# A row softmax on one core: edge columns in eight-row transfers, a written order of work, and the scaling on VectorE

## The chip, the cores and the metric

The kernel runs on one core of one Trainium2 chip. The metric is the device time in microseconds. Before the change it was 2495.66 us, the median of three runs from 2494.19 to 2496.56.

The core's engines work side by side and meet only at semaphores. VectorE (DVE in the profile) and ScalarE (ACT) compute, SyncE (SP) issues the transfers here, and 16 DMA engines move the data between the device memory and the on-chip memory of 128 partitions. TensorE does nothing in this kernel, and GpSimd only sets four constants at the start.

## The reference

The input is 16 x 256 rows of 32768 fp32 values, 4096 rows in all, 536.87 MB. The output has the same shape and type. The temperature is 1.0.

```python
def reference(logits, temperature):
    scaled = logits / temperature
    scaled = scaled - scaled.max(axis=-1, keepdims=True)
    exp_scaled = np.exp(scaled)
    return (exp_scaled / exp_scaled.sum(axis=-1, keepdims=True)).astype(np.float32)
```

## The kernel before

Each row is cut into two halves of 16384 columns, and a half row takes one partition, so that partitions 2r and 2r+1 hold the halves of one row. 128 half rows make a group; there are 64 groups (`G`). A group is worked in two chunks (`C`) of 128 x 8192 values, 4 MB each, so there are 128 chunks, numbered 0 to 127 here. Six buffers of a chunk each (`_BUFS`) hold them. A chunk is loaded into its buffer, changed in place, and stored from it.

For each chunk, `exps` has VectorE find the negated maximum of each partition (line 107, into `nm`), and ScalarE take the exponential with that maximum as bias and add up the results (line 114, the sum into `ssum`). After the two chunks of a group, `factors` puts them together: VectorE takes the extreme of the two maxima (line 129), `combine` swaps neighbouring partitions with a shuffle (line 84) and joins the two (line 87), ScalarE takes the exponentials of the differences (`ee`, line 131), VectorE multiplies them with the sums and adds (line 138), `combine` swaps and joins once more, this time the sums, and a reciprocal (line 149) and a product (line 150) give the factor `f` of each chunk. Then `scales` multiplies the chunk by its factor, the left 4096 columns on VectorE (line 160), the right 4096 on ScalarE (line 163).

All loads (line 64) and stores (line 75) are issued from SyncE, one after the other in the order of the list `order` (lines 170 to 174): six loads, store 0, then store i followed by load i+5. A load waits until the store that last read its buffer, store i-1, has landed. The chunks of the first and the last group are loaded in two pieces of 4096 columns; in the last group the maxima, the exponentials, the scaling and the stores are cut in the same way. The semaphores and the order of the instructions on VectorE and ScalarE are the framework's: `factors` is marked as having priority (line 128).

Of the kernel before, what the change touches and what calls it, by code (L numbers as in the profile page):

```python
# [6 lines left out]


_SPLIT = 2
_CW = 8192  # L10
_BUFS = 6
_PIECE = 8192
_LAST_DMA = 4096
_DVE_SHARE = 0.5


@with_exitstack
def kernel(
    ctx: ExitStack,
    tc: tile.TileContext,  # L20
    logits: bass.AP,
    temperature: bass.AP,
    out: bass.AP,
):
    nc = tc.nc
    inv_t = 1.0 / float(temperature)
    P = nc.NUM_PARTITIONS
    fp32 = mybir.dt.float32
    Exp = mybir.ActivationFunctionType.Exp
    Copy = mybir.ActivationFunctionType.Copy  # L30
    X = mybir.AxisListType.X
    A = mybir.AluOpType

    xf = logits.flatten_outer_dims()
    of = out.flatten_outer_dims()
    N, V = xf.shape
    W = V // _SPLIT
    CW = min(_CW, W)
    C = W // CW
    assert W * _SPLIT == V and CW * C == W and (N * _SPLIT) % P == 0  # L40
    x = xf.rearrange("n (h v) -> (n h) v", h=_SPLIT)
    o = of.rearrange("n (h v) -> (n h) v", h=_SPLIT)
    G = N * _SPLIT // P
    n_chunks = G * C
    n_rounds = _SPLIT.bit_length() - 1

    xpool = ctx.enter_context(tc.tile_pool(name="x", bufs=_BUFS))
    spool = ctx.enter_context(tc.tile_pool(name="stats", bufs=3))
    slots = {}
    stats = {}  # L50

    def spans(total: int, step: int) -> list[tuple[int, int]]:
        return [(s, min(step, total - s)) for s in range(0, total, step)]

    def piece(g: int) -> int:
        return _PIECE if g < G - 1 else min(_PIECE, _LAST_DMA)

    def load(i: int) -> None:
        g, c = divmod(i, C)
        xs = xpool.tile([P, CW], fp32, tag="x", name="xs")  # L60
        slots[i] = xs
        for s, n in spans(CW, _LAST_DMA if g in (0, G - 1) else CW):
            tc.keep_in_program_order(
                nc.sync.dma_start(  # L64
                    out=xs[:, s : s + n],
                    in_=x[g * P : (g + 1) * P, c * CW + s : c * CW + s + n],
                )
            )

    def store(i: int) -> None:  # L70
        g, c = divmod(i, C)
        xs = slots.pop(i)
        for s, n in spans(CW, _LAST_DMA if g == G - 1 else CW):
            tc.keep_in_program_order(
                nc.sync.dma_start(  # L75
                    out=o[g * P : (g + 1) * P, c * CW + s : c * CW + s + n],
                    in_=xs[:, s : s + n],
                )
            )

    def combine(v, op) -> None:
        for j in range(n_rounds):
            mask = [i ^ (1 << j) for i in range(32)]
            nc.vector.stream_shuffle(  # L84
                out=v[:, j + 1 : j + 2], in_=v[:, j : j + 1], mask=mask
            )
            nc.vector.tensor_tensor(  # L87
                out=v[:, j + 1 : j + 2],
                in0=v[:, j : j + 1],
                in1=v[:, j + 1 : j + 2],  # L90
                op=op,
            )

    def exps(i: int) -> None:
        g, c = divmod(i, C)
        xs = slots[i]
        ps = spans(CW, piece(g))
        K = C * len(ps)
        if c == 0:
            stats[g] = tuple(  # L100
                spool.tile([P, K], fp32, tag=f"{nm}{K}", name=nm)
                for nm in ("nm", "ssum", "ee", "f", "ttj")
            )
        nm, ssum = stats[g][:2]
        for j, (s, n) in enumerate(ps):
            k = c * len(ps) + j
            nc.vector.tensor_reduce(  # L107
                out=nm[:, k : k + 1], in_=xs[:, s : s + n], axis=X, op=A.max, negate=True
            )
            if inv_t != 1.0:  # L110
                nc.vector.tensor_scalar_mul(
                    out=nm[:, k : k + 1], in0=nm[:, k : k + 1], scalar1=inv_t
                )
            nc.scalar.activation(  # L114
                out=xs[:, s : s + n],
                in_=xs[:, s : s + n],
                func=Exp,
                bias=nm[:, k : k + 1],
                scale=inv_t,
                accum_out=ssum[:, k : k + 1],  # L120
            )

    def factors(g: int) -> None:
        nm, ssum, ee, f, ttj = stats[g]
        nMh = spool.tile([P, 1 + n_rounds], fp32, tag="nMh", name="nMh")
        Sh = spool.tile([P, 1 + n_rounds], fp32, tag="Sh", name="Sh")
        rS = spool.tile([P, 1], fp32, tag="rS", name="rS")
        with tc.high_priority():
            nc.vector.tensor_reduce(out=nMh[:, 0:1], in_=nm, axis=X, op=A.min)  # L129
            combine(nMh, A.min)  # L130
            nc.scalar.activation(  # L131
                out=ee,
                in_=nm,
                func=Exp,
                bias=nMh[:, n_rounds : n_rounds + 1],
                scale=-1.0,
            )
            nc.vector.tensor_tensor_reduce(  # L138
                out=ttj,
                in0=ee,  # L140
                in1=ssum,
                scale=1.0,
                scalar=0.0,
                op0=A.mult,
                op1=A.add,
                accum_out=Sh[:, 0:1],
            )
            combine(Sh, A.add)
            nc.vector.reciprocal(out=rS, in_=Sh[:, n_rounds : n_rounds + 1])  # L149
            nc.vector.tensor_scalar_mul(out=f, in0=ee, scalar1=rS)  # L150

    def scales(i: int) -> None:
        g, c = divmod(i, C)
        xs = slots[i]
        f = stats[g][3]
        ps = spans(CW, piece(g))
        for j, (s, n) in enumerate(ps):
            k = c * len(ps) + j
            cut = int(n * _DVE_SHARE) // 512 * 512
            nc.vector.tensor_scalar_mul(  # L160
                out=xs[:, s : s + cut], in0=xs[:, s : s + cut], scalar1=f[:, k : k + 1]
            )
            nc.scalar.activation(  # L163
                out=xs[:, s + cut : s + n],
                in_=xs[:, s + cut : s + n],
                func=Copy,
                scale=f[:, k : k + 1],
            )

    order = [("L", i) for i in range(min(_BUFS, n_chunks))] + [("S", 0)]  # L170
    for i in range(1, n_chunks):
        order.append(("S", i))
        if i + _BUFS - 1 < n_chunks:
            order.append(("L", i + _BUFS - 1))

    nxt = 0
    done = -1
    loaded = 0
    for kind, i in order:
        if kind == "L":  # L180
            load(i)
            loaded = i + 1
        else:
            g = i // C
            if g > done:
                while nxt < (g + 1) * C:
                    assert nxt < loaded
                    exps(nxt)
                    nxt += 1
                factors(g)  # L190
                done = g
            scales(i)
            store(i)


# [33 lines left out]
```

## Time and profile before

| | |
|---|---|
| time, median of three runs | 2495.66 us |
| profiled execution: span | 2493.8 us |
| bytes read and written | 536.87 MB each |
| mean rate over the span | 431 GB/s |
| maximum of a chunk, line 107, VectorE | 8.68 us each |
| exponential of a chunk, line 114, ScalarE | 7.12 us each |
| scaling of half a chunk, line 160, VectorE | 2.35 us each |
| scaling of half a chunk, line 163, ScalarE | 3.70 us each |
| load of 4 MB, issue to landing, median | 29.0 us |
| store of 4 MB, issue to landing, median | 38.2 us |

The span is the time from the first to the last instruction of one execution as the hardware profiler recorded it; the time of a run holds a little more than the span. The page gives the busy time of each engine, the share of the 16 DMA engines' time in which they moved packets, and the chain of work that ended last. Groups of instructions are named by line, engine, operation and operands, with the number of instructions, busy time and mean length, and the idle time of the engine ahead of them with what ended it. The DMA share in a window is a mean over the 16 engines, so that 0.50 can mean that eight of them are working. "SPq" is SyncE's own queue, where the issue of a transfer takes 0.34 to 0.53 us and stands behind whatever SyncE waits for.

### The profile page before, as it was taken

The page shows a single profiled execution, that of the slowest core. Times are in us where ns is not written, and L with a number is a line of the kernel's source. Part 1 is how long each engine was busy: PE and PEld are TensorE (multiplying, and loading weights), DVE is VectorE, ACT ScalarE, POOL GpSimd, SP SyncE. Part 2 cuts the span into 40 slices and gives each one's busy share as a digit, 9 for nine tenths or more (in the row PEclk, how much of TensorE's full clock was granted, in tenths as well). Part 3 has the DMA queues.
Part 4 walks back from the last instruction along what each step waited for, and adds up shares of the span by engine and source line. Part 5 has one row for each costly group of instructions (what it writes and reads, how often), then busy time and mean ns, then how long its engine had stood idle before and what let it go on. Part 6 is the DMA issues. An engine that isn't in the chain of part 4 may idle for free.

```text
span 2493.8 us, 2234 instructions
## 1 busy us (share of the span) xinstructions
DVE 1487.4 (60%) x964; ACT 1405.0 (56%) x455; POOL 0.2 (0%) x4
## 2 busy tenths in 40 slices
DVE  7655565556655566555665566655666566655663
ACT  5665554655556555565555655555546555465553
POOL 0000000000000000000000000000000000000000
DMA  9999999999999999999999999999999999999998
GB/s 412 433 430 432 429 431 432 433 433 434 433 434 432 435 432 435 432 435 431 436 431 435 432 434 433 434 433 433 433 433 433 433 433 434 434 433 434 432 431 368
DMA packets 37745, 1073.90 MB, mean 431 GB/s; under 512 B 4192, under 2 KB 4192, under 8 KB 4192
## 3 DMA queue, kind: packets, MB, share of 16 engines
q1 hardware_dynamic: 37728, 1073.76, 99.9%
q14 instruction: 17, 0.14, 0.0%
HBM read 536.87 MB, written 536.87 MB: 431 GB/s over the span
## 4 chain that ended last, share of the span: by engine, by line
DMA 96%; SPq 1%; ACT 1%; DVE 1%; issue 1%; ACTq 0%
DMA out_dram<-xs 93%; DMA xs<-in_logits_dram 2%; SPq L64 1%; DVE nm L107 1%; ACT xs L163 1%; ACT xs L114 0%; ACTq L224 0%; SPq L75 0%; DVE f L150 0%; ACT ee L131 0%; DVE rS L149 0%; DVE Sh L87 0%; DVE ttj L138 0%; DVE Sh L84 0%; DVE Sh L138 0%
## 5 line engine op out<-in xcount | busy, mean ns | idle before, releaser
L114 ACT ACTIVATE xs<-xs,nm 128x8192 f32<-128x8192 f32 (+1 forms) x130 | 912.1, 7016 | 972.4 <-DVE nm L107 972.4
L107 DVE TENSOR_REDUCE nm<-xs 128x1 f32<-128x8192 f32 (+1 forms) x130 | 1111.6, 8551 | 527.3 <-DMA xs<-in_logits_dram 527.3
L163 ACT ACTIVATE xs<-xs,f 128x4096 f32<-128x4096 f32 (+1 forms) x130 | 468.1, 3648 | 71.4 <-DVE f L150 71.4
L160 DVE TENSOR_SCALAR xs<-xs,f 128x4096 f32<-128x4096 f32 (+1 forms) x130 | 295.7, 2318 | 3.7 <-DVE f L150 1.8
L138 DVE CUSTOM_DVE_ANT_0 ttj<-ee,ssum 128x2 f32<-128x2 f32 x64 | 10.3, 161 | 423.8 <-ACT ee L131 423.8
L114 ACT ACTIVATION_READ_ACCUMULATOR xs<-xs,nm 128x1 f32 x130 | 24.2, 186 | 0.0
L131 ACT ACTIVATE ee<-nm,nMh 128x2 f32<-128x2 f32 x64 | 17.9, 280 | 0.0
L150 DVE TENSOR_SCALAR f<-ee,rS 128x2 f32<-128x2 f32 x64 | 14.6, 229 | 2.2
L149 DVE RECIPROCAL rS<-Sh 128x1 f32<-128x1 f32 x64 | 10.5, 164 | 2.2
L87 DVE TENSOR_TENSOR nMh<-nMh 128x1 f32<-128x1 f32 x64 | 10.2, 160 | 2.2
L87 DVE TENSOR_TENSOR Sh<-Sh 128x1 f32<-128x1 f32 x64 | 10.2, 160 | 2.2
L129 DVE TENSOR_REDUCE nMh<-nm 128x1 f32<-128x2 f32 x64 | 9.9, 155 | 2.2
L84 DVE STREAM_SHUFFLE nMh<-nMh 128x1 f32<-128x1 f32 x64 | 9.7, 151 | 0.0
L84 DVE STREAM_SHUFFLE Sh<-Sh 128x1 f32<-128x1 f32 x64 | 9.7, 151 | 0.0
L114 ACT ACT_TABLE_LOAD x1 | 1.3, 1283 | 12.9 <-DMA xs<-in_logits_dram 12.9
L138 DVE DVE_READ_ACCUMULATOR2_ANT Sh<- 128x1 f32 x64 | 5.3, 84 | 0.0
L84 DVE LOAD_MASK_SELECT Sh<-Sh x64 | 0.9, 14 | 2.8
L84 DVE LOAD_MASK_SELECT nMh<-nMh x64 | 0.9, 14 | 2.7
L210 POOL MEMSET const-bfloat16-1.0<- 128x1 bf16 x1 | 0.1, 102 | 0.0
L210 POOL MEMSET const-uint8-127<- 128x1 uint8 x1 | 0.1, 102 | 0.0
L210 POOL MEMSET const-float32-0.0<- 128x1 f32 x1 | 0.1, 99 | 0.2 <-issue 0.2
L210 POOL MEMSET const-float32-1.0<- 128x1 f32 x1 | 0.1, 99 | 0.0
## 6 DMA issues: line engine op xcount, KB each, us to landing
out_dram<-xs SPq DMA_DIRECT2D x126, 4096.0 KB, 38.2
xs<-in_logits_dram SPq DMA_DIRECT2D x124, 4096.0 KB, 29.0
xs<-in_logits_dram SPq DMA_DIRECT2D x8, 2048.0 KB, 22.3
out_dram<-xs SPq DMA_DIRECT2D x4, 2048.0 KB, 26.7
```

What stands on the lines that cost most here:

```text
L64: nc.sync.dma_start(out=xs[:, s : s + n], in_=x[g * P : (g + 1) * P, c * CW + s : c * CW + s + n],)
L84: nc.vector.stream_shuffle(out=v[:, j + 1 : j + 2], in_=v[:, j : j + 1], mask=mask)
L87: nc.vector.tensor_tensor(out=v[:, j + 1 : j + 2], in0=v[:, j : j + 1], in1=v[:, j + 1 : j + 2], op=op,)
L107: nc.vector.tensor_reduce(out=nm[:, k : k + 1], in_=xs[:, s : s + n], axis=X, op=A.max, negate=True)
L114: nc.scalar.activation(out=xs[:, s : s + n], in_=xs[:, s : s + n], func=Exp, bias=nm[:, k : k + 1], scale=inv_t, accum_out=ssum[:, k : k + 1],
L129: nc.vector.tensor_reduce(out=nMh[:, 0:1], in_=nm, axis=X, op=A.min)
L131: nc.scalar.activation(out=ee, in_=nm, func=Exp, bias=nMh[:, n_rounds : n_rounds + 1], scale=-1.0,)
L138: nc.vector.tensor_tensor_reduce(out=ttj, in0=ee, in1=ssum, scale=1.0, scalar=0.0, op0=A.mult, op1=A.add, accum_out=Sh[:, 0:1],)
L149: nc.vector.reciprocal(out=rS, in_=Sh[:, n_rounds : n_rounds + 1])
L150: nc.vector.tensor_scalar_mul(out=f, in0=ee, scalar1=rS)
L160: nc.vector.tensor_scalar_mul(out=xs[:, s : s + cut], in0=xs[:, s : s + cut], scalar1=f[:, k : k + 1])
L163: nc.scalar.activation(out=xs[:, s + cut : s + n], in_=xs[:, s + cut : s + n], func=Copy, scale=f[:, k : k + 1],)
```

## The change

The function is written anew, outside the framework's scheduling.

- Every engine's instructions stand in the order in which they are written, and each wait is written out by `Stream.wait`. Each engine has a semaphore of its own that counts its instructions; each buffer has semaphores of its own for its loads and its stores (`Landing`).
- In a group VectorE does, in this order: the maxima of both chunks; after the last exponential one shuffle that swaps maxima and sums together; the extreme over both halves; after `ee` the product-sum over both halves; the reciprocal; the scaling of both chunks. There is one exchange between the partitions in place of two, and no product `f`.
- The scaling is one VectorE instruction for the whole chunk with two scalar operands, `ee` and the reciprocal. ScalarE scales nothing.
- SyncE issues six loads, then for each group, after its stores in order, load i+4 behind store i. Load i+4 goes into the buffer that store i-2 read.
- The last 2048 columns of chunk 5 (the sixth) are loaded by 16 transfers, each of 8 partitions that are 4 apart, all on one semaphore of that buffer. The first 6144 columns are one transfer.

```diff
-    order = [("L", i) for i in range(min(_BUFS, n_chunks))] + [("S", 0)]
-    for i in range(1, n_chunks):
-        order.append(("S", i))
-        if i + _BUFS - 1 < n_chunks:
-            order.append(("L", i + _BUFS - 1))
...
+    for i in range(_BUFS):
+        load(i)
+    for g in range(G):
+        compute(g)
+        for c in range(C):
+            i = g * C + c
             store(i)
+            j = i + _LEAD
+            if j >= _BUFS and j < n_chunks:
+                load(j)
+    sp.wait(*[s.token() for s in stores])
```

Inside `load`, with `_NARROW` = 2048 and `_LEAD` = 4:

```diff
+        b = i % _BUFS
+        sp.wait(*freed[b])
+        pieces = spans(_CW, _EDGE if g in (0, G - 1) else _CW)
+        narrow = _NARROW if i == _BUFS - 1 else 0
+        if narrow:
+            pieces = [(0, _CW - narrow)]
...
+            for q in range(0, P, 32):
+                for r in range(4):
+                    a = q + r
+                    lane.add(
+                        nc.sync.dma_start(
+                            out=X[a : a + 29 : 4, b * _CW + s : (b + 1) * _CW],
+                            in_=x[g * P + a : g * P + a + 29 : 4, c * _CW + s : (c + 1) * _CW],
+                        )
+                    )
```

The exchange and the scaling, in `compute`. Here `t` holds the maxima and then the sums of a group's pieces, `K` of each, and `tv` is a view of it that separates own and neighbour's, maxima and sums:

```diff
+        dve.wait(sums[-1])
+        sh = dve.done(
+            nc.vector.stream_shuffle(out=t[:, 2 * K : 4 * K], in_=t[:, 0 : 2 * K], mask=swap)
+        )
+        dve.wait(sh)
+        mx = dve.done(
             nc.vector.tensor_reduce(
+                out=r[:, 0:1], in_=tv[:, :, 0, :], axis=mybir.AxisListType.XY, op=A.min
+            )
+        )
+        act.wait(mx)
...
+        dve.wait(tr)
+        rc = dve.done(nc.vector.reciprocal(out=r[:, 2:3], in_=r[:, 1:2]))
+        dve.wait(rc)
+        for c in range(C):
...
+                scaled[i, s] = dve.done(
+                    nc.vector.tensor_scalar(
+                        out=xs,
+                        in0=xs,
+                        scalar1=e[:, k : k + 1],
+                        scalar2=r[:, 2:3],
+                        op0=A.mult,
+                        op1=A.mult,
+                    )
+                )
```

And the helper that every wait goes through; a value that the engine has already waited for is not waited for again:

```diff
+    def wait(self, *tokens):
+        need = {}
+        for t in tokens:
+            for sem, value in t if isinstance(t, list) else [t]:
+                key = id(sem)
+                if value > max(self.seen.get(key, 0), need.get(key, (None, 0))[1]):
+                    need[key] = (sem, value)
+        for key, (sem, value) in need.items():
+            self.engine.wait_ge(sem, value)
+            self.seen[key] = value
```

## The prediction

> **What bounds the kernel now.** I read the page first, then the stretches of the span in windows, then the end in 1 us windows, then the queue of SyncE and the first 90 us in order of time.
>
> ```profile
> span 2493.8 us, 2234 instructions
> DVE 1487.4 (60%) x964; ACT 1405.0 (56%) x455; POOL 0.2 (0%) x4
> q1 hardware_dynamic: 37728, 1073.76, 99.9%
> DMA out_dram<-xs 93%; DMA xs<-in_logits_dram 2%; SPq L64 1%; DVE nm L107 1%; ACT xs L163 1%; ACT xs L114 0%; ACTq L224 0%; SPq L75 0%; DVE f L150 0%; ACT ee L131 0%; DVE rS L149 0%; DVE Sh L87 0%; DVE ttj L138 0%; DVE Sh L84 0%; DVE Sh L138 0%
> ```
>
> The transfers are 99.9% of the span of 16 DMA engines, and the chain that ended last is 93% store. VectorE and ScalarE, at 60% and 56%, are not the bound. So only two things can move the end: the rate of the DMA engines, and how evenly the sixteen reach the last byte. The windows (columns: stretch, length, DVE busy, ACT busy, POOL busy, clock, DMA share, GB/s):
>
> ```profile
> 62.00:150.00 88.00, 54.13 (x40) 58.90 (x21) 0.00 (x0) 1.00 1.00 431
> 150.00:470.00 320.00, 190.39 (x121) 175.38 (x56) 0.00 (x0) 1.00 1.00 431
> 470.00:1000.00 530.00, 320.80 (x210) 299.74 (x97) 0.00 (x0) 1.00 1.00 433
> ...
> 2481.00:2482.00 1.00, 0.00 (x0) 0.00 (x0) 0.00 (x0) 1.00 0.96 410
> 2482.00:2483.00 1.00, 0.00 (x0) 0.00 (x0) 0.00 (x0) 1.00 0.50 213
> 2485.00:2486.00 1.00, 0.00 (x0) 0.00 (x0) 0.00 (x0) 1.00 0.42 180
> 2487.00:2488.00 1.00, 0.00 (x0) 0.00 (x0) 0.00 (x0) 1.00 0.15 66
> 2491.00:2492.00 1.00, 0.00 (x0) 0.00 (x0) 0.00 (x0) 1.00 0.08 33
> ```
>
> The steady rate is 433 GB/s: 1073.74 MB would take 2479.8 us, and from a first byte near 2.5 us the end would be 2482.3. At that very time the share drops to 0.50: eight of sixteen engines are done, two are left at 2487.5 (0.15 x 16), one at 2491.5. The last engine is some 10 us behind the first eight. The ten 1 us shares after 2482 (0.50, 0.54, 0.42, 0.42, 0.19, 0.15, 0.12, 0.04, 0.08, 0.08) add up to 2.5, so level engines would end near 2484.5, 7.5 us earlier. That uneven end is all there is to gain. Most of it comes from the first fifth: 431 instead of 433 over 88 and 320 us is 0.4 + 1.5 = 1.9 us for the mean engine, three quarters of the 2.5.
>
> Profile and times: the span is 1.9 us below the median of the runs (2495.66) and 0.4 below the lowest. I add 1.9 to each span I work out.
>
> **Part 1: written order and earlier stores in the queue.** Before, load i+5 follows store i and waits for store i-1; after, load i+4 follows store i and waits for store i-2. A wait at the head of SyncE holds all behind it, stores and loads. Steadily, when load 2g+1 has landed, four transfers stand ahead of store 2g (store, load, store, load; 4 x 4.194 MB / 433 = 38.7 us). The store needs a maximum, an exponential, the exchange and one scaling, for which the rows are:
>
> ```profile
> L107 DVE TENSOR_REDUCE nm<-xs 128x1 f32<-128x8192 f32 x126 | 1094.0, 8682 | 523.4 <-DMA xs<-in_logits_dram 523.4
> L114 ACT ACTIVATE xs<-xs,nm 128x8192 f32<-128x8192 f32 x126 | 897.2, 7121 | 965.1 <-DVE nm L107 965.1
> L160 DVE TENSOR_SCALAR xs<-xs,f 128x4096 f32<-128x4096 f32 x126 | 290.8, 2350 | 3.7 <-DVE f L150 1.8
> ```
>
> 8.7 + 7.1 + 0.2 (accumulator read) + 1.25 + 4.5 = 21.8 us, 17 us in hand: cost 0. At the end, behind the last load only stores 124 and 125 (19.4 us) cover the last group's first store, which needs 4.4 + 3.7 + 0.2 + 1.3 + 2.4 = 12.0 for its halves of a chunk: 7 in hand, cost 0. If that cover went, the queue would run dry and each us late would be a us of span.
>
> **Part 2: one exchange.** Two shuffles, two tensor_tensor and the product f (0.15 + 0.15 + 0.16 + 0.16 + 0.23) go; one wider shuffle and a reduction over both halves come. Before, from the last accumulator read of a group (end 85.91) to the end of f (87.15) is 1.24 us with 0.2 per small step; after, shuffle, maximum, ee (0.28), product-sum (0.22), reciprocal, with a hop each way, are about 1.25. Gain 0: it lies beside DMA. The written waits sit before small steps that waited for their predecessor already; the rows' 0.2 steps include that.
>
> **Part 3: scaling on VectorE alone.** 128 copies of 3.7 us leave ScalarE. VectorE scales 8192 columns: 2 x 2.35 less one start, 4.5 us. The form with two scalar operands is not in the trace. Bounds: 4.5 at the pace of L160, 8.7 at that of L107 (one element per cycle, the same columns). L160 is the nearer row, same operation and operand kinds, so 4.5. VectorE's group in its written order is 2 x 8.7 + 7.3 + 1.25 + 2 x 4.5 = 35.0 of 38.7 us: 3.7 in hand, cost 0. The maxima of the next group are now queued behind both scalings; before, one stood between them.
>
> **Part 4: the start.** Before, the maxima of chunk 2 ran ahead of the scaling; now they are behind both scalings.
>
> ```profile
> 12.89 8.69 DVE L107 TENSOR_REDUCE nm<-xs 128x1 f32<-128x8192 f32 x1 [12.89 <-DMA xs<-in_logits_dram]
> 22.68 8.69 DVE L107 TENSOR_REDUCE nm<-xs 128x1 f32<-128x8192 f32 x1 [1.10 <-DMA xs<-in_logits_dram]
> 38.43 0.19 ACT L114 ACTIVATION_READ_ACCUMULATOR xs<-xs,nm 128x1 f32 x1
> ...
> 75.22 0.33 SPq L75 DMA_DIRECT2D out_dram<-xs  x1
> 81.93 0.34 SPq L64 DMA_DIRECT2D xs<-in_logits_dram  x1
> ```
>
> From 38.6: + 1.25 + 4.5 gives store 0 at 44.4 (before 51.9), store 1 at 48.9; then 2 x 8.7 + 7.3 + 1.25 + 4.5 gives store 2 at 79.4 (before 75.2). Load 6 stands behind it on SyncE and goes at 79.8 (before 71.9). The data queued ahead, six loads and two stores, ends at 81.9: the issue at 81.93 is the one that store 1's landing released. A first byte takes some 1.5 us from the issue (first issue 0.73, first bytes near 2.3), so store 2's come at 80.9: 1 us in hand, so no hole for engines with an even load. Bounds 0 and 3 us, if a small step costs more here than in the rows; I take 0.
>
> **Part 5: sixteen transfers of 8 rows.** 1 MB of chunk 5 is cut off. Issues: 16 x 0.34 to 0.53 us = 5.4 to 8.5 us on SyncE, after 8 issues that end at 4.7; SyncE has nothing else until 44, so 0. The page's 37728 packets are 262 transfers x (128 rows + 16 small): one packet to a row. Eight rows cannot occupy more than eight engines at once. Evenly rotated over all sixteen, the MB costs the 2.4 us it costs now. If the same eight take all of it, they get 4.8 us of work in place of 2.4, the others none: the eight end 2.4 us later, the others 2.4 earlier, 4.8 apart. If one engine takes it all, 1.05 MB at 433/16 GB/s are 38.8 us: + 36. I take the eight. A row-to-packet count gives no engine numbers, so for the last engine this term is -2.4 or +2.4. The relieved eight run dry at 79.5 and wait to 80.9 for store 2: 1.4 of their 2.4 is lost again, and -1.0 is left; the halves are then 3.4 apart.
>
> The Trainium skill (DMA: Bandwidth & Descriptors, Why a DMA increments its semaphore by 16 and not by 1) says an 8-row transfer from SyncE uses the lowest-numbered eight engines; this trace has no such transfer, and by the page the term is the 2.4 either way. Against the change, the same page's Rules for kernel authors would have transfers of 64 KB merged, and its table in Bandwidth gives 0.95 us for one: an estimate of 15 us for sixteen in a row. The row here, 99.9% with transfers queued behind each other, speaks for no such gap, and by the page the start would be 13 us longer.
>
> With the halves 3.4 to 4.8 us apart, loads of one half meet stores of the other from the start, the state that the old kernel drifts into while it runs at 431; after 470 us, drifted apart, it runs at 433. So I expect less of the early lag. Bounds for the last engine: -5.7 (three quarters of the 7.5) and +3, as much again as half of that, if halves out of step hinder each other for longer. I take -4.5, near the good end, since 433 with engines apart is what four fifths of the span show.
>
> **Sum.** 2493.8 - 1.0 (late engines relieved) - 4.5 + 0 for the other parts = 2488.3 of span, + 1.9 = 2490.2, forecast 2490.
>
> **Rivals.**
> 1. *The late engines are the loaded ones, or the early lag stays.* For: nothing in the trace says which eight end at 2482. + 2.4 - 4.5 gives 2493.6; - 1.0 with no less lag 2494.7; rotated over all engines, so that the halves are not set apart at all, 2495.7. No change.
> 2. *Store 2 is late.* The slower side. If VectorE's first two groups need 6 us more than worked out (3 in each), all sixteen engines run dry, load 6 queued behind store 2 as it is. From a store 2 issued at 86, 6.6 us late, first bytes at 87.5, 5.6 after 81.9; the 2.4 of the loaded engines is absorbed in that, all start level again, and the old lag grows: 2495.7 + 5.6 = 2501.3. It decides, past 0.2%, from an issue at 85.4. For: only 1 us in hand; against: every length is a row of the trace. The halves hindering each other by 3 with + 2.4 would be 2501.1 too.
> 3. *VectorE becomes the bound.* At 8.7 us a scaling, the group takes 43.4, 4.7 over 38.7: 62 x 4.7 + 12 at the start, near 2800. It decides from 6.3 us a scaling. Against: L160 runs at two elements per cycle.
>
> **Chances.** Forecast 0.47 (2487 to 2491), rival 1 0.35 (2491 to 2497), rival 2 0.11 (2498 to 2505), rival 3 0.05, one engine loaded 0.02. Range: low 2486, a little under - 2.4 - 5.7 (2487.6) because the number of lagging engines may fall as well; high 2499, which takes in rival 1 and the small holes of rival 2 and leaves out rival 3; the forecast's own range is 2486 to 2491. About 0.2%, 5 us, is what a measurement of this kernel can tell from no change. Faster (below 2490.7) 0.45, same 0.37, slower (above 2500.7) 0.18.
>
> **What would show it.** DMA share still 99% over the span and 433 GB/s in the steady windows; 433, not 431, between 150 and 470; the share after 2482 falling within 5 us; issue of store 2 near 79, scaling rows of 4.5 us; no slice below 0.95 near 80. Wrong: scaling rows above 6 us, VectorE above 90%, a dip at 82, or the share reaching 0.1 as long after 0.5 as before.

## The result, and the profile after

The changed kernel takes 2497.64 us, the median of 20 runs (2495.55 to 2501.14); the kernel before took 2494.72 in 20 runs beside it. The ratio is 1.0013, with a 95% interval of 1.0007 to 1.0019: 2.9 us slower, by less than the 0.2% that was set for a change to count, and on the other side of zero from the forecast. The profiled execution took 2497.24 us with a span of 2495.5, 1.7 more than the span of the kernel before.

The page of the changed kernel, its totals, the rate in 40 slices, and the two costly lines of VectorE:

```profile
span 2495.5 us, 1305 instructions
DVE 1723.7 (69%) x644; ACT 944.5 (38%) x325; POOL 0.2 (0%) x4
GB/s 411 417 422 430 431 434 433 432 435 432 435 431 436 430 436 431 435 434 431 435 431 436 431 435 430 435 435 431 435 431 435 431 436 430 436 433 432 436 430 374
q1 hardware_dynamic: 37984, 1073.76, 99.9%
L173 DVE TENSOR_REDUCE t<-xs 128x1 f32<-128x8192 f32 (+1 forms) x130 | 1111.1, 8551 | 257.6 <-DMA xs<-in_logits_dram 257.6
L238 DVE TENSOR_SCALAR xs<-xs,ee,row 128x8192 f32<-128x8192 f32 (+1 forms) x130 | 576.5, 4478 | 2.3
```

The DMA engines are still the bound at 99.9%, and VectorE has room at 69%. A scaling of 8192 columns takes 4.5 us (the 4478 ns of the row include four half chunks). What differs is the second and third slice, 417 and 422 GB/s, where the kernel before has 433 and 430. The same in windows (stretch, length, DVE busy, ACT busy, POOL busy, clock, DMA share, GB/s), first the kernel before, then the changed one:

```profile
78.00:82.00 4.00, 0.99 (x5) 4.00 (x2) 0.00 (x0) 1.00 0.93 401
82.00:102.00 20.00, 14.08 (x10) 12.97 (x6) 0.00 (x0) 1.00 1.03 442
102.00:210.00 108.00, 59.55 (x44) 59.87 (x20) 0.00 (x0) 1.00 1.00 430
210.00:470.00 260.00, 154.08 (x93) 143.07 (x46) 0.00 (x0) 1.00 1.00 432
```

```profile
78.00:82.00 4.00, 4.00 (x2) 0.00 (x0) 0.00 (x0) 1.00 0.77 328
82.00:102.00 20.00, 18.87 (x3) 8.31 (x3) 0.00 (x0) 1.00 1.02 406
102.00:210.00 108.00, 77.11 (x30) 43.08 (x15) 0.00 (x0) 1.00 1.00 425
210.00:470.00 260.00, 179.69 (x70) 95.87 (x33) 0.00 (x0) 1.00 1.00 432
470.00:2400.00 1930.00, 1337.53 (x500) 736.27 (x250) 0.00 (x0) 1.00 1.00 433
...
2482.00:2488.00 6.00, 0.00 (x0) 0.00 (x0) 0.00 (x0) 1.00 0.97 415
2488.00:2496.00 8.00, 0.00 (x0) 0.00 (x0) 0.00 (x0) 1.00 0.13 57
```

Between 78 and 82 there is a dip to a share of 0.77, and up to 210 us the engines move less although their share is 1.00 or more. From 210 to 2400 us both kernels are alike. The end is shorter: in the kernel before the share falls to half at 2482 and lasts to 2492, here all engines work to 2488 and a few to 2494. So the engines finish closer together, as was expected, but nearly all of them finish later.

What brings them together is not the start. The trace also holds the time at which each of the sixteen engines' parts of a transfer landed. In the table, store k is the store of chunk k, and the gap is the time between the eighth and the ninth part to land:

| | store 0 | store 2 | store 18 | store 125 | last store |
|---|---|---|---|---|---|
| kernel before, first to last part | 0.46 us | 0.60 us | 5.78 us | 10.46 us | 10.45 us |
| changed kernel, first to last part | 5.17 us | 2.99 us | 6.85 us | 9.55 us | 5.83 us |
| changed kernel, gap | 4.44 us | 2.29 us | 4.49 us | 4.48 us | 0.01 us |
| changed kernel without eight-row transfers (first experiment), first to last part | 0.48 us | 0.62 us | 5.52 us | 5.55 us | 5.45 us |

Up to store 125 the engines of the changed kernel lie nearly as far apart as before, in two blocks of eight. The early eight then run out of work near 2464, because the first store of the last group is issued only at 2467.49, and this wait closes the gap:

```profile
2464.00:2465.00 1.00, 0.56 (x5) 0.30 (x1) 0.00 (x0) 1.00 0.46 197
2465.00:2466.00 1.00, 0.96 (x2) 0.00 (x0) 0.00 (x0) 1.00 0.46 197
2466.00:2467.00 1.00, 1.00 (x1) 0.00 (x0) 0.00 (x0) 1.00 0.53 229
```

```profile
2467.49 7.30 SPq L145 DMA_DIRECT2D out_dram<-xs  x4
```

### The profile page after: what moved, and what is told of

Same layout as the page of the kernel before. It is cut to its first block, busy times and chain, and to the rows that moved or that the text cites. A ratio compares the mean times of both kernels' runs of the same rounds, so it can differ in the third digit from the quotient of the medians.

```text
span 2495.5 us, 1305 instructions
## 1 busy us (share of the span) xinstructions
DVE 1723.7 (69%) x644; ACT 944.5 (38%) x325; POOL 0.2 (0%) x4
## 3 DMA queue, kind: packets, MB, share of 16 engines
q1 hardware_dynamic: 37984, 1073.76, 99.9%
## 4 chain that ended last, share of the span: by engine, by line
DMA 71%; DVE 20%; ACT 7%; issue 0%; another core or an unknown queue 0%; SPq 0%; DVEq 0%
DMA xs<-in_logits_dram 40%; DMA out_dram<-xs 32%; DVE t L173 10%; DVE xs L238 9%; ACT xs L187 7%; ACT ee L211 0%; DVE row L229 0%; DVE row L204 0%; DVE t L200 0%; DVE junk L217 0%; SPq L117 0%; DVE row L217 0%; SPq L145 0%; SPq L290 0%
## 5 line engine op out<-in xcount | busy, mean ns | idle before, releaser
L187 ACT ACTIVATE xs<-xs,t 128x8192 f32<-128x8192 f32 (+1 forms) x130 | 912.1, 7016 | 1492.2 <-DVE t L173 1492.2
L173 DVE TENSOR_REDUCE t<-xs 128x1 f32<-128x8192 f32 (+1 forms) x130 | 1111.1, 8551 | 257.6 <-DMA xs<-in_logits_dram 257.6
L238 DVE TENSOR_SCALAR xs<-xs,ee,row 128x8192 f32<-128x8192 f32 (+1 forms) x130 | 576.5, 4478 | 2.3
L211 ACT ACTIVATE ee<-t,row 128x4 f32<-128x4 f32 x64 | 19.0, 297 | 27.0 <-DVE row L204 27.0
L217 DVE CUSTOM_DVE_ANT_1 junk<-ee,t 128x4 f32<-128x4 f32 x64 | 10.4, 163 | 23.3 <-ACT ee L211 23.3
L187 ACT ACTIVATION_READ_ACCUMULATOR xs<-xs,t 128x1 f32 x130 | 24.2, 186 | 0.0
L229 DVE RECIPROCAL row<-row 128x1 f32<-128x1 f32 x64 | 10.5, 164 | 2.2
L204 DVE TENSOR_REDUCE row<-t 128x1 f32<-128x4 f32 x64 | 10.1, 157 | 2.2
L200 DVE STREAM_SHUFFLE t<-t 128x4 f32<-128x4 f32 x64 | 9.9, 154 | 0.0
L217 DVE DVE_READ_ACCUMULATOR2_ANT row<- 128x1 f32 x64 | 5.3, 82 | 0.0
```

Of the source, the lines that this page charges most:

```text
L173: nc.vector.tensor_reduce(out=t[:, k : k + 1], in_=xs, axis=mybir.AxisListType.X, op=A.max, negate=True)
L187: nc.scalar.activation(out=xs, in_=xs, func=Exp, bias=t[:, k : k + 1], scale=inv_t, accum_out=t[:, K + k : K + k + 1],)
L200: nc.vector.stream_shuffle(out=t[:, 2 * K : 4 * K], in_=t[:, 0 : 2 * K], mask=swap)
L204: nc.vector.tensor_reduce(out=r[:, 0:1], in_=tv[:, :, 0, :], axis=mybir.AxisListType.XY, op=A.min)
L211: nc.scalar.activation(out=ev, in_=tv[:, :, 0, :], func=Exp, bias=r[:, 0:1], scale=-1.0)
L217: nc.vector.tensor_tensor_reduce(out=j_[:, 0 : 2 * K].rearrange("p (a k) -> p a k", a=2), in0=ev, in1=tv[:, :, 1, :], scale=1.0, scalar=0. ...
```

## The experiments

Each time is a median, and each ratio is against the kernel before, run on the same chip beside it (its medians there are 2494.50 to 2494.72). The windows come from one profiled execution of each kernel. Theory A was formed after the result: the eight-row transfers give eight engines 2.4 us more work, and the dip near 80 us takes back what the other eight are spared. Its rival B blamed the written order.

**Without the eight-row transfers.** Chunk 5 in one transfer, all else as changed.

```diff
-        narrow = _NARROW if i == _BUFS - 1 else 0
+        narrow = 0
```

> The changed kernel with chunk 5 loaded in one transfer. Theory A (the eight-row transfers put 2.4 us on eight engines, and the hole ahead of store 2 near 80 us takes the other eight's relief back, so the 2.4 stays on the path): the start has no hole, since even engines run dry only at 81.9, and the time falls by 1 to 3 us, to 0 to +1 us against the kernel before. Theory B (the written order and the later loads alone cost the 3 us; the eight-row transfers are neutral or help): time stays 3 us or more above the kernel before.

2493.41 us (2491.52 to 2496.80, 11 runs), ratio 0.9995 (0.9986 to 1.0004): 4.2 us below the changed kernel, more than the 1 to 3 of theory A, and not to be told from the kernel before. The written order, the single exchange, the scaling on VectorE and the later loads together cost nothing that can be measured. The windows show where the 4.2 us were:

```profile
78.00:82.00 4.00, 4.00 (x2) 0.00 (x0) 0.00 (x0) 1.00 0.99 426
82.00:102.00 20.00, 18.87 (x3) 8.31 (x3) 0.00 (x0) 1.00 0.98 418
102.00:210.00 108.00, 80.15 (x30) 43.08 (x15) 0.00 (x0) 1.00 1.01 432
```

Against the changed kernel this is 98, 12 and 7 GB/s more over 4, 20 and 108 us, or 0.9 + 0.6 + 1.7 = 3.2 us of work of all engines. By the landings of store 125 the mean part is 2.6 us later in the changed kernel (2468.37 against 2465.80; the five kernels with one queue and no eight-row transfers lie between 2465.60 and 2467.08) and the last part 5.6 us. VectorE's and SyncE's times are the same in both, so the late store 2 makes a dip only where eight engines have been relieved.

**An earlier store 2**, with the eight-row transfers kept. ScalarE scales chunk 1 with the product of the two factors, so that VectorE is free 4.5 us earlier.

```diff
+                if g == 0 and c == 1:
+                    ff = dve.done(nc.vector.tensor_scalar_mul(
+                        out=r[:, 3:4], in0=e[:, k : k + 1], scalar1=r[:, 2:3]))
+                    act.wait(ff)
+                    scaled[i, s] = act.done(nc.scalar.activation(
+                        out=xs, in_=xs, func=mybir.ActivationFunctionType.Copy, scale=r[:, 3:4]))
+                    continue
```

> The changed kernel with chunk 1 scaled by ScalarE, so that VectorE is free 4.5 us earlier and store 2 is issued near 75 instead of 79. Theory A: the DMA share has no dip between 79 and 81, the halves stay 4.8 us apart as the eight-row transfers left them, the first windows (62 to 150) rise from 423 to about 428 GB/s and the time falls by 2 to 5 us, below the kernel before by 0 to 2. Theory B: the dip goes, the time moves by less than 1 us.

2496.22 us, ratio 1.0007 (0.9999 to 1.0016): 1.4 us below the changed kernel, not 2 to 5. Store 2 is issued at 74.92 and the dip is gone, as theory A said, but the rate that it expected did not come:

```profile
78.00:82.00 4.00, 4.00 (x2) 0.00 (x0) 0.00 (x0) 1.00 0.91 393
82.00:102.00 20.00, 14.53 (x2) 12.65 (x3) 0.00 (x0) 1.00 1.00 421
102.00:210.00 108.00, 75.55 (x30) 38.75 (x15) 0.00 (x0) 1.00 1.01 418
210.00:470.00 260.00, 181.45 (x70) 95.86 (x33) 0.00 (x0) 1.00 1.00 433
```

With nothing to bring the halves together again (the gap at store 2 is 4.46 us here, 2.29 in the changed kernel), 102 to 210 us falls to 418 from 425. The dip was a small part of the cost, and theory A lacked a term: with the halves out of step, all engines lose time up to 210 us.

**Neither**, the earlier store 2 without eight-row transfers.

> Neither eight-row transfers nor the late store 2. Theory A: as without the eight-row transfers alone, within 1 us, since even engines had no hole; the engines drift apart as in the kernel before, so about the time of the kernel before. Theory B: 3 us above the kernel before.

2493.57 us, ratio 0.9994 (0.9985 to 1.0002).

```profile
82.00:102.00 20.00, 14.50 (x2) 12.67 (x3) 0.00 (x0) 1.00 1.01 433
102.00:210.00 108.00, 80.69 (x30) 38.92 (x16) 0.00 (x0) 1.00 1.00 430
```

It differs from the run above only in the transfers: 2.7 us of time (the intervals just overlap), and 12 GB/s over 20 us and 12 over 108, or 3.6 us of all engines.

**The kernel before with only the eight-row transfers added.** This was to be the change by itself.

```diff
+        if i == _BUFS - 1:
+            pieces = [(0, CW - 2048)]
...
+        if i == _BUFS - 1:
+            s = CW - 2048
+            for q in range(0, P, 32):
+                for r in range(4):
+                    a = q + r
+                    tc.keep_in_program_order(
+                        nc.sync.dma_start(
+                            out=xs[a : a + 29 : 4, s:CW],
+                            in_=x[g * P + a : g * P + a + 29 : 4, c * CW + s : (c + 1) * CW],
+                        )
+                    )
```

> The kernel before with only the load of chunk 5 changed: 6144 columns in one transfer, 2048 in sixteen of eight rows. It has no hole at the start (store 2 goes at 75). Theory A: halves 4.8 us apart from the start, with little further drift up to 470 us; 1 to 4 us faster than the kernel before. Theory B' (the loaded eight carry their 2.4 us to the end and the others drift as before): 2 us slower than the kernel before.

2507.09 us, ratio 1.0052 (1.0038 to 1.0065), far from either. It tells nothing on the tilt, since another wait came in. SyncE's own waits and its queue in this kernel (columns: waited for, us, times, longest; then start, us, instruction):

```profile
SPq L78 <- DMA xs<-in_logits_dram: 49.8, 8, 9.1
59.82 5.30 SPq L78 DMA_DIRECT2D xs<-in_logits_dram  x8
```

```profile
59.00:61.00 2.00, 2.00 (x1) 2.00 (x1) 0.00 (x0) 1.00 0.47 180
61.00:63.00 2.00, 2.00 (x1) 1.86 (x3) 0.00 (x0) 1.00 0.31 98
63.00:65.00 2.00, 1.89 (x7) 0.50 (x1) 0.00 (x0) 1.00 0.35 98
```

The last eight of the sixteen transfers each waited for the landing of an earlier load, so they were issued at 59.8 when the queue was running out, and the rate fell to 98 GB/s. In the changed kernel all sixteen share one semaphore of their own and are issued from 4.9 to 19.8 us without a wait.

**Small transfers without a tilt.** The same 2048 columns in eight transfers of 16 rows.

```diff
-            for q in range(0, P, 32):
+            for q in range(0, P, 64):
...
-                            out=X[a : a + 29 : 4, b * _CW + s : (b + 1) * _CW],
+                            out=X[a : a + 61 : 4, b * _CW + s : (b + 1) * _CW],
```

> The changed kernel with the same 2048 columns in eight transfers of 16 rows (4 apart) in place of sixteen of 8: still small transfers of 8 KB rows, but a row for each of sixteen engines, so nothing tilts the load. Theory A (the cost is that eight engines do double work and are set apart from the others): no dip at 79 to 81, first windows as without small transfers (62 to 150 at 430 or more), time within 1 us of the run with one transfer for chunk 5, that is 0 to 2 us below the kernel before. Rival S (small transfers and their issues cost time as such, whatever engines they fall on): time stays 2 to 4 us above the run with one transfer.

2493.97 us, ratio 0.9998 (0.9989 to 1.0007); 431 GB/s from 102 to 210 and no dip at 78 to 82 (426). Rows of 8 KB in small transfers cost nothing that can be measured; rival S falls. It is the eight rows.

**Chunk 0 in eight-row transfers.** All 4 MB of it, to see how many engines such transfers use.

```diff
+        if i == 0:
+            for a in list(range(0, 4)) + list(range(32, 36)) + list(range(64, 68)) + list(range(96, 100)):
+                loads[0][0].add(nc.sync.dma_start(
+                    out=X[a : a + 29 : 4, 0:_CW], in_=x[a : a + 29 : 4, 0:_CW]))
+            pieces = []
```

> The changed kernel without the edge columns' transfers, and chunk 0 (4 MB) loaded in sixteen transfers of eight whole rows, before anything else. If eight rows always fall on the same eight engines (theory A), the DMA share is 0.5 and the rate about 216 GB/s while these run alone, unless the next loads, queued behind, start on the other eight, which then land far ahead; chunk 0 lands near 2 + 4.19 MB / 216 = 21 us instead of 12.9. If they rotate over sixteen, share 1.0 and chunk 0 lands near 13.

```profile
5.00:10.00 5.00, 0.00 (x0) 0.00 (x0) 0.00 (x0) 1.00 0.52 203
10.00:15.00 5.00, 0.00 (x0) 0.00 (x0) 0.00 (x0) 1.00 0.68 236
20.00:25.00 5.00, 0.00 (x0) 0.00 (x0) 0.00 (x0) 1.00 1.02 210
30.00:50.00 20.00, 15.43 (x2) 7.21 (x2) 0.00 (x0) 1.00 1.00 406
```

As long as only these transfers run, half of the engines work, at 203 GB/s: sixteen transfers in turn do not rotate. The Trainium skill (DMA: Bandwidth & Descriptors, Why a DMA increments its semaphore by 16 and not by 1) says that a transfer issued from SyncE runs on as many engines, at most sixteen, as its rows can be divided among evenly, and on the lowest-numbered ones, so eight for eight rows; the share of 0.52 agrees with the eight, and no run here shows the numbers. Chunk 0 landed at 33.65, not at 21: once the other loads joined on the other engines (share 1.02), the rate stayed at 210, for a reason that is open. The single run took 2513.02 us.

**More and less tilt**, with the earlier store 2: 4096 and 1024 columns in the eight-row transfers.

```diff
-_NARROW = 2048
+_NARROW = 4096
```

> The run with the earlier store 2, and 4096 columns in eight-row transfers in place of 2048: 4.8 us more work for the loaded eight engines, 4.8 less for the others, halves 9.7 us apart, one whole transfer. Theory A with the mean loss between 90 and 210 us due to halves that are out of step: loaded engines end 2.4 us later than with 2048 columns, time 2 to 5 us above the run with 2048. Rival R (only the 2.4 us per MB matters and the loss of 90 to 210 us is not from being out of step): plus 2.4, and the windows 102 to 210 at 430.

> The early store 2, with 1024 columns in eight-row transfers: 1.2 us of tilt each way, halves 2.4 us apart. Theory A with a loss that depends on how far the halves are apart: windows 102 to 210 between those of no tilt (430) and of 2048 columns (418), time 0.5 to 2.5 us above the run with neither. If the loss comes from any tilt at all: 418 as with 2048.

| columns in eight-row transfers | halves apart | gap at store 2, store 18 | GB/s, 102 to 210 us | time | ratio (95%) |
|---|---|---|---|---|---|
| 0 | 0 | 0.04, 0.16 us | 430 | 2493.57 | 0.9994 (0.9985 to 1.0002) |
| 1024 | 2.4 us | 2.52, 4.70 us | 422 | 2494.68 | 1.0000 (0.9991 to 1.0009) |
| 2048 | 4.8 us | 4.46, 6.13 us | 418 | 2496.22 | 1.0007 (0.9999 to 1.0016) |
| 4096 | 9.7 us | 8.46, 5.34 us | 428 | 2495.03 | 1.0001 (0.9992 to 1.0010) |

Halves apart is worked out from the bytes, the gap is read from the landings. The expectation for 1024 came true. That for 4096 missed: the time is 1.2 us under that with 2048, not 2 to 5 above it, though eight engines carry 2.4 us more. The times alone do not tell the rows with a tilt apart, since their intervals overlap; the rates do, as the six kernels with one queue and no tilt at the start lie between 430 and 432. The loss is largest at 4.8 us, half a transfer of 9.7, and nearly gone at a whole one. Neither the bytes nor the number of transfers does that (1024, 2048 and 4096 have sixteen each); what is left is how the halves stand to each other.

Being apart does not cost for good: from 470 to 2400 us all four move 433 GB/s, while the gaps of the lower three stay at 4.7, 6.1 and 5.3 us up to store 125. The loss lies in the first few hundred us, in which the gaps move towards these values. That this movement is what costs is a reading of these rows and was not tested by itself.

**Fewer changeovers.** If the loss is where some engines load and others store already, fewer changes between the two should help: two stores, then two loads, per group, without eight-row transfers.

```diff
             store(i)
-            j = i + _LEAD
+        for c in range(C):
+            j = g * C + c + _LEAD
```

> No eight-row transfers, early store 2, and SyncE's order changed from store, load, store, load to store, store, load, load within a group: half as many changes between loading and storing. Theory A (time is lost where some engines still load while others store already): the windows 102 to 470 rise from 430-432 to 432-433, the share falls from 0.5 to 0.1 within 4 us at the end, and the time falls by 1 to 3 us below the run with neither. Rival Q (the early loss has another cause): within 1 us of that run.

2494.95 us, ratio 1.0002 (0.9993 to 1.0011), 1.4 us above the run with neither (the intervals overlap). The windows from 102 to 470 show 430 and 431, not 433. The theory in that simple form falls: fewer changeovers do not mean less loss.

**The tilt at the end.** The last 2048 columns of store 125 in eight-row transfers, none at the start.

```diff
+        if i == n_chunks - 3:
...
+            for q in range(0, P, 32):
+                for a in range(q, q + 4):
+                    stores[b].add(nc.sync.dma_start(
+                        out=o[g * P + a : g * P + a + 29 : 4, (c + 1) * _CW - 2048 : (c + 1) * _CW],
+                        in_=X[a : a + 29 : 4, (b + 1) * _CW - 2048 : (b + 1) * _CW]))
```

> No eight-row transfers at the start, early store 2, and instead the last 2048 columns of store 125 in sixteen eight-row transfers: the eight engines of these transfers get 2.4 us more, the others 2.4 less, with nothing after it but the last four stores. If the engines that end last are among those the eight-row transfers use, the time rises by 2 to 3 us over the run with neither; if they are among the others, it falls by 1 to 2.4 us. Rival (eight-row transfers spread over all sixteen): no change.

2495.23 us, ratio 1.0002 (0.9993 to 1.0011), 1.7 us above the run with neither. The intervals overlap; it points to late engines among the eight that carry the double work, which is the wrong side for the change.

**No changeovers at all.** Stores from ScalarE's queue, loads from SyncE's, no eight-row transfers.

```diff
-            sp.wait(scaled[i, s])
+            act.wait(scaled[i, s])
             stores[b].add(
-                nc.sync.dma_start(
+                nc.scalar.dma_start(
```

> The changed kernel without eight-row transfers, its stores issued from ScalarE's queue instead of SyncE's, so that loads and stores share each DMA engine packet by packet instead of changing over every 9.7 us. If the loss between 60 and 470 us is at the changeovers, the windows 102 to 470 rise to 433 and the time falls by 1 to 4 us below the run with one transfer for chunk 5. If the engines' pace depends on the mix itself, the steady windows move off 433 in either direction, 10 us or more of time per 2 GB/s.

2497.75 us, ratio 1.0012 (1.0004 to 1.0021). The early loss is gone, and the end is lost in another way:

```profile
102.00:210.00 108.00, 80.51 (x30) 48.39 (x16) 0.00 (x0) 1.00 1.01 434
...
2460.00:2465.00 5.00, 2.81 (x1) 0.00 (x0) 0.00 (x0) 1.00 0.60 259
2465.00:2470.00 5.00, 1.61 (x1) 3.36 (x1) 0.00 (x0) 1.00 0.03 13
2470.00:2475.00 5.00, 4.04 (x8) 0.74 (x3) 0.00 (x0) 1.00 0.10 43
2475.00:2480.00 5.00, 5.00 (x3) 0.00 (x0) 0.00 (x0) 1.00 1.02 429
```

434 GB/s from 102 to 210, where every kernel with one queue had 418 to 432. But the stores, in a queue of their own, no longer stand behind the last loads: loads and stores are through together at 2464, and the last group's arithmetic has nothing beside it: from the shares, 2.0 + 4.9 + 4.5 = 11.4 us of empty engines between 2460 and 2475.

**The same, with the last four stores behind the last load.**

```diff
-            act.wait(scaled[i, s])
+            q = sp if i >= n_chunks - _LEAD else act
+            q.wait(scaled[i, s])
             stores[b].add(
-                nc.scalar.dma_start(
+                q.engine.dma_start(
```

> The run with stores on ScalarE's queue, but the last four stores (124 to 127) issued from SyncE behind the last load, and no eight-row transfers. In the run with all stores on ScalarE's queue the last loads landed only at 2462 and the DMA share fell to 0.03 to 0.10 between 2465 and 2475: about 12 us of hole at the end. If that hole is what hid the gain of the rate without changeovers, the last loads land near 2445, the hole goes, all engines end within 2 us near 2484, and the time is 2485 to 2488, 7 to 9 us below the kernel before. Rival: a lag of single engines comes back, 2490 to 2493.

2490.73 us (2490.04 to 2491.51, 11 runs), ratio 0.9985 (0.9976 to 0.9994): 4.0 us below the kernel before, and faster than both kernels, though by less than the 0.2% and short of the 2485 to 2488 that were expected. Against the run with one transfer for chunk 5 (0.9986 to 1.0004) the gain is not clear of the noise.

```profile
102.00:210.00 108.00, 80.51 (x30) 48.39 (x16) 0.00 (x0) 1.00 1.00 432
2460.00:2470.00 10.00, 7.68 (x4) 0.00 (x0) 0.00 (x0) 1.00 1.00 429
...
2480.00:2482.00 2.00, 0.00 (x0) 0.00 (x0) 0.00 (x0) 1.00 0.95 410
2482.00:2484.00 2.00, 0.00 (x0) 0.00 (x0) 0.00 (x0) 1.00 0.19 82
2486.00:2488.00 2.00, 0.00 (x0) 0.00 (x0) 0.00 (x0) 1.00 0.04 16
```

The hole is filled. After 2482 the share is 0.19 at once, three engines of sixteen, where the kernel before has 0.50: eight. One engine is left until 2488, so part of the rival came true: the lag of single engines stays, and it is what still separates the time from 2485.

**The same with the eight-row transfers back.** The difference to the run above is `narrow` alone.

> The same with the sixteen eight-row transfers of the changed kernel. Loads and stores are mixed packet by packet here, so there is no changeover at which halves out of step could hinder each other. If the cost of the transfers is the tilt plus that hindrance, only the tilt is left: the halves end about 5 us apart and the time is 2.4 us, 2 to 3, above the run without them. If the whole 3 to 4 us come back, the hindrance has another cause than the changeovers; if nothing, the tilt is evened out by the two queues.

The profiled execution has a span of 2492.1 against 2488.9, and in it the windows

```profile
62.00:102.00 40.00, 25.57 (x11) 17.62 (x7) 0.00 (x0) 1.00 1.02 424
102.00:210.00 108.00, 83.47 (x31) 44.15 (x15) 0.00 (x0) 1.00 1.00 433
```

The 418 to 425 GB/s up to 210 us do not come back after the start, where 424 remain from 62 to 102: in this execution, with mixed queues, the tilt then costs no rate, as expected. It is the shortest of the twelve. The others go up to 2685.06, with a median of 2555.81, for a reason that was not sought, so nothing can be read from the time, the windows speak for the one execution alone, and the 2.4 us of pure tilt could not be measured by itself.

## Why the prediction was wrong

The bound, the offset of span and time (1.9 taken, 1.7 found) and most of the arithmetic held. The forecast failed on the two terms that gave it its sign.

- **Part 1, order and queue.** Cost 0, shown: without the eight-row transfers the ratio is 0.9995. One cover was thinner than worked out. The last group's first store was to have 7 us in hand; it was issued at 2467.49, and from 2464 to 2467 the share is 0.46 to 0.53: the early eight engines were dry. The maxima of chunk 126 stood behind two scalings, and a load counts as landed only when its latest engine is done. It cost the late engines, which set the end, nothing: from the last part of store 125 to the last part of all it is 19.42 us in both kernels.
- **Part 2, one exchange.** 1.25 us taken. From the last accumulator read (end 38.93) to the scaling (40.08) it took 1.15. Cost 0.
- **Part 3, scaling.** 4.5 us taken, 4.54 found for a whole chunk; VectorE stays in its cover. Rival 3 is out.
- **Part 4, the start.** Store 2 was worked out for 79.4 and came at 79.25. The dip of the relieved eight was taken as 1.4 us of eight engines; 0.9 us of all sixteen against the run without the transfers is 1.8 of eight, and the gap in the landings falls by 2.2, from 4.48 at store 1 to 2.29 at store 2. The 1.5 us from an issue to the first byte was too little for a queue that has run dry, and was misread besides: the kernel before moves its first packets at 1.75, not near 2.3. A size a little off, and the dip itself was one of the prediction's own signs of being wrong. Rival 2, a store 2 that is 6 us late, is out.
- **Part 5, the issues.** 14.85 us in place of 5.4 to 8.5; hidden, since the first store goes at 44.65. The sixteen landed between 59.5 and 65.0, in 5.4 us on their eight engines, so the estimate of 15 us for them in a row did not come true.
- **Part 5, the tilt.** Eight engines, 2.4 us each way: the eight are shown. For the last engine I took "-1.0 (late engines relieved)"; the loaded engines were the late ones. The gap that the transfers opened (4.44 us at store 0) is still there at store 125 (4.48), so the loaded eight stayed behind all the way, and the run with the tilt at the end points the same way. The prediction had both signs and nothing in the profile to choose by; the choice was a guess and should have been counted as one.
- **Part 5, the halves apart: the step that failed.** I wrote that the halves out of step are "the state that the old kernel drifts into while it runs at 431; after 470 us, drifted apart, it runs at 433", and took -4.5 from it, "near the good end". The runs showed the opposite: 430 with halves in step, 418 with halves 4.8 us apart, 428 at 9.7 apart. Where -4.5 was taken, the loss against the run with one transfer is 3.2 us of all engines by the windows and 2.6 by the landings of store 125, near the bad bound of +3. The state that it read was right: from 470 to 2400 us the changed kernel too moves 433 GB/s, with its halves 4.5 us apart. What failed is the way there, which was taken as free: a state reached by drifting says what no longer costs, not what it costs to be set into it. Nor did the halves end the drift inside them, since from the first to the last part it is 5.17 us at store 0 and 9.55 at store 125.

Summed: between the profiled executions with and without the transfers the spans differ by 5.7 us (2495.5 and 2489.8) and the last parts of store 125 by 5.6, of which 2.6 are common to the mean of the sixteen and the rest, 3.1 before rounding, is the last engine's own. Tilt and dip together are in that rest; the 2.4 from the bytes was not measured by itself. The medians differ by 4.2, in part because the execution without the transfers was the second shortest of its eleven. That the cost comes from the tilt is shown by the runs with 16 rows and with one transfer, and by the rates with 1024 to 4096 columns. That it arises where loading and storing meet on one queue is supported by the two runs with separate queues, at 432 to 434 GB/s against 430 to 432, and by one execution in which the loss does not return there with the tilt, but it is not shown: the run with two loads and two stores in a row speaks against the simple count of changeovers. What inside the DMA engines makes them slow each other is open.

## What to carry to other kernels

Where transfers fill the span, look at how the engines end, not only at their mean share: a share that falls from 0.5 to 0.04 over 10 us was nearly the whole gain that was left here. Before moving work between engines, find out which of them are late; a transfer of eight rows loads only eight engines, and setting them out of step slowed all sixteen here until about 210 us. A rate that holds in a settled stretch does not tell what the way into that state costs. Loads and stores on two queues kept thirteen of sixteen engines level (and with the eight-row transfers scattered the time up to 2685 us), but then the last group needs its stores held back behind the last load, or its arithmetic stands bare at the end.

## What the runs showed of the hardware that was not expected

- Sixteen DMA engines at a share of 1.00 move 418 to 434 GB/s between 102 and 210 us in these kernels, which differ there in how eight of them stand to the other eight and in whether loads and stores share a queue.
- The loss is not in proportion to the distance: 422, 418 and 428 GB/s at 2.4, 4.8 and 9.7 us; and it ends, with 433 GB/s from 470 us on at gaps of 4.7 to 6.1 us.
- Sixteen engines that start 0.46 us apart drift to 10.46 us in the kernel before without any tilt (landings of stores 0 and 125).
- The Trainium skill (DMA: Bandwidth & Descriptors, Rules for kernel authors) says that spreading transfers over the issuing engines does not help bandwidth and saves issue time only. Here the steady rate is indeed 433 either way, but with stores on ScalarE's queue the windows from 102 to 470 show 432 to 434 where one queue without a tilt has 430 to 432, thirteen engines end level, and with the end mended the time is 0.15% (interval 0.06% to 0.24%) below that of the kernel before. The queue's own share in that is not clear of the noise.
- Eight-row transfers of whole rows held the rate at 210 GB/s even with all engines at work beside them (share 1.02 from 20 to 25 us).
